# A hybrid attention and feed-forward block: another order of seven down-projection products, constant products at the start, and a later broadcast and rotary table

## The chip, the cores and the metric

The kernel runs on one core of one Trainium2 chip. The time is device microseconds (us) of one execution, from the kernel's start to its end; lower is better. The profile is that of one execution on the chip.

## The reference, cut to what matters

One layer (DEPTH is 1), 512 positions of width 2048, all float32. The products carry full float32 precision in the kernel, by way of split operands.

```python
h = rmsnorm(x, g_attn_pre)
proj = h @ w_in                       # [stick-breaking q | k | v | latents | rotary key]
o_sb  = stick_breaking_attention(q_sb, k_sb, v_sb)
o_mla = mla_attention(q_nope, apply_rope(q_rope, cos, sin), k_nope, apply_rope(k_rope, cos, sin), v)
mixed = concat(rmsnorm(o_sb), rmsnorm(o_mla))
x = x + rmsnorm(mixed @ w_o, g_attn_post)
h = rmsnorm(x, g_ffn_pre)
u = causal_depthwise_conv(h @ w_up, conv_w, conv_b)       # w_up: 2048 x 11264
gate, val = split(u)
y = (gelu(gate) * val) @ w_down                            # w_down: 5632 x 2048
x = x + rmsnorm(y, g_ffn_post)
```

## The kernel before

The engines are TensorE (PE), VectorE (DVE), ScalarE (ACT), GpSimd (POOL) and SyncE (SP, which issues loads). Every float32 operand is split into a high and a low part (`hi`, `lo`) of TensorE's rounded float32 type, and every product is three matmuls: high by high, and the two mixed ones (`three`, L119 to L122). A weight tile is loaded by an SP transfer into `wr` (raw), ScalarE casts it to `wh` (L109, L921), and VectorE subtracts to get `wl` (L111, L921). A tile framework puts each engine's instructions into a fixed order, which each engine then runs through in that order; `tc.issue_after` (wrapped as `behind`, L116) pins an instruction behind another one.

**The start.** `gen_v(0)` makes the values of the first heads: 16 k-steps of 12 matmuls, each 128x128 by 128x512, in four banks. Its weights come as two tiles of one k-step and seven of two, each k-step with a 256 KB row of the transposed x (`x_rows`), which is scaled and split into `act_hi` (ScalarE, L194) and `act_lo` (VectorE, L195). When all k-steps but the last are written, `x_squares` loads x a second time in 16 tiles `acc` (five buffers) and sums their squares on ScalarE (L201). From these come the norms: a reduction (L481), a power on GpSimd, the scales `sx` and `nsx` (L485, L486) and the diagonal tile `t` (L139). The products are made with x that isn't normed; the norm comes in when the banks are copied out (L325, L326). Then `gen_qk(0)` makes q and k of the first pair, 16 k-steps of 6 matmuls; after its first k-step, two full-float32 matmuls broadcast the norm from `t` to all partitions (`bcast`, L145, copied out by L146). `rope_tables` (L382 and on) computes cosine and sine for the rotary parts, mostly on VectorE in tiles `aT`.

**Middle.** Both attentions, `w_o`, and the up-projection. The last goes in units: a block product is made from seven block products instead of eight (`sevenfold`, L928), with sums and differences of blocks on both sides. After the last products of one unit, the left sides of the first down-projection chunk are made (`then`, in `up_steps`).

**The down-projection.** `open_down` (L1079) makes room: `act_lo` for left sides, and twenty 128x512 pages for sums: `u2`, `11`, `12`, `21` and `22`. There are five chunks (`NST`) and in each two halves `q` of the columns. In each half the seven products of `sevenfold` are made with an accumulating variant: 24 matmuls of 128x128 by 128x512 each. `quarter` loads a weight block of 1 MB on SP; `added` adds another block onto a raw tile with an accumulating transfer that GpSimd issues. `wr` has four buffers, `wh` and `wl` three. `g_side` (L1107) makes the left side of product n for a chunk out of four blocks that are loaded into `a5h` and `a5l`: a copy (ScalarE, L1123), a subtraction (VectorE, L1124), for some also a difference of blocks (VectorE, L1129). The left sides sit in `a6h` (product 1), `a6l` (2), `a3h` (5), `s6` (6; shown as `s`), `a3l` (7) and `act_lo` (3, 4). `down_steps` (L1161) names the bank pairs and what follows each product:

```python
    ORDER = (1, 2, 5, 6, 7, 3, 4)
        name = {1: "X", 2: "X", 5: "D", 3: "D", 7: "C", 4: "C", 6: "Y"}[n]
        fresh = n in (1, 5, 7, 6)
```

A fresh product overwrites its banks; products 2, 3 and 4 add onto the banks of 1, 5 and 7. After each product `add_to` (L1088) adds its banks to the pages: product 1 to `u2` (by ScalarE's copy, L1092, in the first chunk, by VectorE, L1094, later), product 2 to `11`, and so on. In half 1 of a chunk, the left side of product n of the next chunk is made right after product n.

**The end.** `open_last` (L1205) adds and subtracts `u2` to and from the pages of the other sums (twelve operations, L1219, L1223 and L1224). `last_steps` makes the last two blocks' products, in 16 groups of 12 matmuls, each taken from its bank by VectorE (L1243); then come the norm, the residual and the output.

## Time and profile before

| | |
|---|---|
| median of 3 runs | 2044.94 us (2043.98 to 2048.38) |
| profiled execution, its own time | 2040.72 us |
| span of its instructions | 2038.9 us |
| TensorE busy | 2003.2 us (98%) |
| VectorE busy | 1532.6 us (75%) |
| ScalarE busy | 924.4 us (45%) |
| mean granted TensorE clock | 0.998 of full speed |
| last matmul begins | 2027.87 us |

The span runs from the first to the last instruction. In a row of the timeline the columns are: start in us, duration in us, engine, source line, operation, output and inputs by the names in the program with their shapes, how many stand in the row, and in brackets how long the engine idled before it and what it waited for. Matmuls overlap, so their distance, not their duration, says what one costs. In the list of waits, a row gives the engine, the waiting tile and line, the releaser, and the total in us, the number of times and the longest. In a table of windows, a row gives the stretch, its length, and the busy time (with the number of instructions) of TensorE, its weight load, VectorE, ScalarE and GpSimd, then the granted clock, the share of the transfer engines and GB/s.

### The profile page before, as it was taken

What the parts mean: (1) busy time and instruction counts of PE and PEld (TensorE: products, weight loads), DVE (VectorE), ACT (ScalarE), POOL (GpSimd) and SP (SyncE); (2) the same over time, 40 slices, a digit from 0 to 9 for tenths busy, and PEclk for the clock granted to TensorE, in tenths of its full rate; (3) what the DMA queues carried; (4) which work ended last, traced back from release to release, by engine and by line L of the source; (5) the groups of instructions that cost most, each with busy time, mean ns of one, the idle gap of its engine ahead of it and who ended that gap; (6) DMA issues with size and microseconds to landing.
All of it is one profiled execution on the core that took longest, in us unless ns stands there. A gap on an engine that the chain in (4) does not pass through costs nothing.

```text
span 2038.9 us, 29849 instructions
## 1 busy us (share of the span) xinstructions
PE 2003.2 (98%) x12580; PEld 1808.4 (89%) x12580; DVE 1532.6 (75%) x1556; ACT 924.4 (45%) x1105; POOL 159.6 (8%) x192
## 2 busy tenths in 40 slices
PE   9999999999999999999999999999999999999997
PEld 7788888888888889999999999999999788878876
DVE  7454355687343888888888888888888889898886
ACT  6343244466433654454444444444444564444432
POOL 0000000123021200000000000000000000000004
PEclk9999999999999999999999999999999999999999
DMA  8422322211532524224323432343235677767772
GB/s 277 125 73 74 103 73 65 81 42 63 181 122 99 177 95 133 94 94 148 132 94 99 159 115 94 114 154 105 94 129 187 180 189 203 206 169 183 207 206 83
DMA packets 186630, 266.12 MB, mean 131 GB/s; under 512 B 8832, under 2 KB 123648, under 8 KB 185984
## 3 DMA queue, kind: packets, MB, share of 16 engines
q1 hardware_dynamic: 170704, 227.04, 34.2%
q0 software_dynamic: 15360, 36.71, 8.2%
q8 instruction: 98, 1.61, 0.3%
q10 hardware_dynamic: 432, 0.47, 0.1%
q14 instruction: 36, 0.29, 0.0%
HBM read 244.26 MB, written 19.92 MB: 130 GB/s over the span
## 4 chain that ended last, share of the span: by engine, by line
PE 82%; DVE 9%; DMA 3%; issue 3%; ACT 3%; POOL 0%; SPq 0%; DVEq 0%; ACTq 0%; POOLq 0%
PE ps L984 40%; PE ps L1156 10%; PE ps L120 9%; PE ps L121 9%; PE ps L122 9%; PE ps L270 2%; DVE wl L921 2%; ACT wh L921 1%; DMA wr<-in_w_down_dram 1%; PE ps L865 1%; DVE wr L925 1%; PE ps L246 1%; DVE act_hi L1094 1%; DVE t L452 0%; DVE wl L111 0%
## 5 line engine op out<-in xcount | busy, mean ns | idle before, releaser
L921 ACT CAST wh<-wr 128x2048 fp32r<-128x2048 f32 x220 | 419.0, 1909 | 613.5 <-DVE wr L925 274.1
L921 DVE TENSOR_TENSOR wl<-wr,wh 128x2048 fp32r<-128x2048 f32 x220 | 503.1, 2288 | 149.6 <-ACT wh L921 149.4
L984 PE MATMUL ps<-act_hi,wh 128*128 128x256 f32 x1344 | 380.4, 283 | 1.6 <-ACT wh L921 1.6
L984 PE MATMUL ps<-act_hi,wl 128*128 128x256 f32 x1344 | 380.4, 283 | 0.0
L984 PE MATMUL ps<-act_lo,wh 128*128 128x256 f32 x1344 | 380.4, 283 | 0.0
L111 DVE TENSOR_TENSOR wl<-wr,wh 128x1024 fp32r<-128x1024 f32 (+2 forms) x107 | 130.3, 1218 | 185.1 <-ACT wh L109 184.8
L984 PEld LDWEIGHTS ps<-act_hi,wh 128*128 128x128 f32 x1344 | 258.0, 192 | 1.9 <-ACT wh L921 1.8
L984 PEld LDWEIGHTS ps<-act_lo,wh 128*128 128x128 f32 x1344 | 258.0, 192 | 0.0
L984 PEld LDWEIGHTS ps<-act_hi,wl 128*128 128x128 f32 x1344 | 258.0, 192 | 0.0
L925 DVE TENSOR_TENSOR wr<-wr 128x2048 f32<-128x2048 f32 x104 | 237.7, 2286 | 1.1
L109 ACT CAST wh<-wr 128x1024 fp32r<-128x1024 f32 (+2 forms) x107 | 110.3, 1031 | 200.4 <-PE ps L121 78.3
L122 PE MATMUL ps<-wh,act_lo 128*128 128x512 f32 x400 | 156.2, 390 | 0.0
L120 PE MATMUL ps<-act_hi,wh 128*128 128x512 f32 x368 | 145.2, 395 | 0.0
L122 PE MATMUL ps<-act_hi,wl 128*128 128x512 f32 x368 | 143.4, 390 | 0.0
L121 PE MATMUL ps<-act_lo,wh 128*128 128x512 f32 x368 | 143.4, 390 | 0.0
L120 PE MATMUL ps<-wh,act_hi 128*128 128x512 f32 x352 | 138.1, 392 | 5.0 <-ACT act_hi L194 5.0
L121 PE MATMUL ps<-wl,act_hi 128*128 128x512 f32 x352 | 137.5, 391 | 0.0
L1156 PE MATMUL ps<-wh,act_lo 128*128 128x512 f32 x320 | 100.4, 389 | 0.7 <-ACT act_hi L1092 0.7
L984 PE MATMUL ps<-a5h,wl 128*128 128x256 f32 x336 | 95.2, 283 | 1.5 <-DVE wl L921 1.5
L984 PE MATMUL ps<-a6h,wl 128*128 128x256 f32 x336 | 95.1, 283 | 0.0
L984 PE MATMUL ps<-a5h,wh 128*128 128x256 f32 x336 | 95.1, 283 | 0.0
L984 PE MATMUL ps<-a3h,wh 128*128 128x256 f32 x336 | 95.1, 283 | 0.0
(392 smaller groups left out, 4351.9 us busy)
## 6 DMA issues: line engine op xcount, KB each, us to landing
wr<-in_w_up_dram SPq DMA_DIRECT2D x84, 1024.0 KB, 6.5
wr<-in_w_down_dram SPq DMA_DIRECT2D x44, 1024.0 KB, 6.9
wr<-in_w_in_dram SPq DMA_DIRECT2D x59, 512.0 KB, 3.7
wr<-in_w_down_dram POOLq DMA_DIRECT2D x20, 1024.0 KB, 9.7
wr<-in_w_o_dram SPq DMA_DIRECT2D x32, 512.0 KB, 3.6
g_dram<-v POOLq DMA_DIRECT2D x42, 256.0 KB, 6.0
a5l<-g_dram SPq DMA_DIRECT2D x5, 1024.0 KB, 11.0
a5h<-g_dram SPq DMA_DIRECT2D x5, 1024.0 KB, 8.3
```

Source lines behind the costliest of these rows:

```text
L109: sc.copy(hi, raw)
L111: ve.tensor_tensor(lo, raw, f(hi), ALU.subtract)
L120: te.matmul(ps, lh, rh, start=start, stop=False)
L121: te.matmul(ps, lh, rl, start=False, stop=False)
L122: seen["mm"] = te.matmul(ps, ll, rh, start=False, stop=stop)
L246: te.transpose(dst, a(b, j), ident)
L270: te.matmul(dst, q[:, b * P:(b + 1) * P], k[:, k0:S], start=i == 0, stop=False)
L865: mark["part"] = te.matmul(dst, l[:, kk, ms], r, start=first and kg == 0 and kk == 0 and i == 0, stop=kg == 3 and kk == 3 and i == 2, skip ...
L921: made.append((sc.copy(hi, w), ve.tensor_tensor(lo, w, f(hi), ALU.subtract)))
L925: ve.tensor_tensor(w, w, v, ALU.add)
L984: te.matmul(dst, l[:, k, ms], r[:, k, :], start=fresh and k == 0 and m == 0 and i == 0, stop=k == 7 and i == 2, skip_group_check=True)
L1156: te.matmul(bs[t], l[:, k, ts_], r[:, k, :], start=fresh and k == 0 and i == 0, stop=k == FU - 1 and i == 2, skip_group_check=True)
```

## The change

Seven edits. (1) `ones` is filled first on GpSimd, and nine products of it with itself go into a bank that nothing reads. (2) The first weights of `gen_v(0)` come as four tiles of one k-step and six of two; the raw tiles of the four lie in pages of other tags. (3) The rotary table's first operation stands behind the last `lo` of the first values, not behind `act_lo` of k-step 4. (4) Six k-steps of `gen_qk(0)` instead of one stand before the broadcast. (5) The down-projection's products come in the order 1, 5, 2, 6, 7, 3, 4. (6) The left sides of the first chunk: 1, 5 and 2 are made after products 6, 7 and 3 of the last up unit, 6 after product 1 of the first half (`open_sixth`), 7 after 5, 3 after 2, 4 after 6; before, 6, 7, 3 and 4 all came after the last product of the up unit. (7) The twelve `u2` operations of `open_last` stand behind the last `wl`.

```diff
--- before.py
+++ after.py
@@ -71,12 +71,15 @@
     def f(t):
         return t.bitcast(F32)
 
+    ones = const.tile([P, P], F32, name="ones")
+    po.memset(ones, 1.0)
+    idle = bank()
+    for _ in range(9):
+        te.matmul(idle[:, 0:P], ones, ones, start=True, stop=True)
     ident = const.tile([P, P], F32, name="ident")
     make_identity(nc, ident)
     identb = const.tile([P, P], BF16, name="identb")
     po.tensor_copy(identb, ident)
-    ones = const.tile([P, P], F32, name="ones")
-    po.memset(ones, 1.0)
     sbmask = const.tile([P, P], BF16, name="sbmask")
     po.memset(sbmask, 0.0)
     po.affine_select(out=sbmask, in_=sbmask, pattern=[[1, P]], compare_op=ALU.is_gt, fill=NEG,
@@ -102,8 +105,8 @@
     def new_raw(shape):
         return wp.tile(shape, F32, tag="wr", name="wr", bufs=2)
 
-    def load_w(src, r0, kn, c0, cols):
-        raw = new_raw([P, kn, cols])
+    def load_w(src, r0, kn, c0, cols, raw=None):
+        raw = new_raw([P, kn, cols]) if raw is None else raw
         sy.dma_start(raw, src[r0:r0 + kn * P, c0:c0 + cols].rearrange("(k p) c -> p k c", p=P))
         hi = wp.tile([P, kn, cols], R32, tag="wh", name="wh")
         sc.copy(hi, raw)
@@ -304,10 +307,11 @@
 
     def gen_v(vb, first=False):
         banks = [bank() for _ in range(NT)]
-        steps = [1, 1] + [2] * 7 if first else [2] * 8
+        steps = [1] * 4 + [2] * 6 if first else [2] * 8
         for kg, kn in enumerate(steps):
             k0 = sum(steps[:kg])
-            wh, wl = load_w(w_in, k0 * P, kn, 2 * SBW + vb * 512, 512)
+            raw = page("s" if kg < 2 else "om", 3).rearrange("p (k c) -> p k c", k=1) if kn == 1 else None
+            wh, wl = load_w(w_in, k0 * P, kn, 2 * SBW + vb * 512, 512, raw)
             if first:
                 for kk in range(kn):
                     x_rows(k0 + kk)
@@ -323,7 +327,7 @@
         for t in range(NT):
             hi, lo = pg_v(R32), pg_v(R32)
             sc.activation(hi, banks[t], AF.Copy, scale=rx[:, t:t + 1])
-            ve.scalar_tensor_tensor(lo, banks[t], rx[:, t:t + 1], f(hi), ALU.mult, ALU.subtract)
+            seen["v"] = ve.scalar_tensor_tensor(lo, banks[t], rx[:, t:t + 1], f(hi), ALU.mult, ALU.subtract)
             v_sb[vb].append((hi, lo))
 
     qk_sb = {}
@@ -386,7 +390,7 @@
         def tmp():
             return pg_at()
         ang, a1, a2 = tmp(), tmp(), tmp()
-        with behind(("lo", 4)):
+        with behind("v"):
             ve.tensor_copy(ang, posi)
         ve.tensor_scalar_mul(ang, ang, gcol(C_INVF, 0))
         m12, m22 = MAGIC * 2.0 ** 12, MAGIC * 2.0 ** 22
@@ -487,7 +491,7 @@
     run(vgen)
     rx_d = diagonals(rx)
     qk0 = gen_qk(0)
-    run(qk0, 1.0)
+    run(qk0, 7.7)
     with behind("mm"):
         rx_bc = bcast(rx_d, page("rx", 1))
     cos, ssin = rope_tables()
@@ -964,7 +968,7 @@
             return w_parts(w[11] if added else plus(w[11], w[21]))
 
         if added:
-            return p1, p2, p5, p6, p7, p3, p4
+            return p1, p5, p2, p6, p7, p3, p4
         return p1, p5, p6, p7, p2, p3, p4
 
     later = []
@@ -1052,7 +1056,7 @@
         def then(use, *ns):
             def both(w):
                 use(w)
-                if ns[0] == 6:
+                if not ns:
                     open_down()
                 for n in ns:
                     g_side(0, n)
@@ -1060,8 +1064,8 @@
             return both
 
         if unit == NFF // 2 - 1:
-            return zip(sevenfold(quarter, (8, 256)), (m1, m5, then(m6, 1), then(m7, 2), m2, then(m3, 5),
-                                            then(m4, 6, 7, 3, 4)))
+            return zip(sevenfold(quarter, (8, 256)), (m1, m5, then(m6, 1), then(m7, 5), m2, then(m3, 2),
+                                            then(m4)))
         return zip(sevenfold(quarter, (8, 256)), (m1, m5, m6, m7, m2, m3, m4))
 
 
@@ -1076,10 +1080,13 @@
     def kept(name, shape, dt=F32):
         return hp.tile([P, *shape], dt, tag=name, name=name)
 
-    def open_down():
+    def open_sixth():
         some(len(later))
         tp_stack.close()
         d["gp"], d["gpool"] = stacked("gp", side="right")
+        g_side(0, 6)
+
+    def open_down():
         d["rest"] = kept("act_lo", (16, S), R32)
         ps = pages(kept("act_hi", (16, S))) + [pg_v() for _ in range(4)]
         d["acc"] = {n: {(t, q): ps.pop(0) for q in range(2) for t in range(2)}
@@ -1156,7 +1163,7 @@
                     te.matmul(bs[t], l[:, k, ts_], r[:, k, :], start=fresh and k == 0 and i == 0,
                               stop=k == FU - 1 and i == 2, skip_group_check=True)
 
-    ORDER = (1, 2, 5, 6, 7, 3, 4)
+    ORDER = (1, 5, 2, 6, 7, 3, 4)
 
     def down_steps(ch, q):
         def rows(kh, nh):
@@ -1183,6 +1190,9 @@
             down_product(z[name], w, d["g"][n], fresh)
             if q == 1 and ch + 1 < NST:
                 g_side(ch + 1, n)
+            if first and q == 0:
+                {1: open_sixth, 5: lambda: g_side(0, 7), 2: lambda: g_side(0, 3),
+                 6: lambda: g_side(0, 4)}.get(n, lambda: None)()
             if n == 1:
                 add_to("u2", q, z["X"], first)
             elif n == 2:
@@ -1212,16 +1222,17 @@
                 ve.tensor_tensor(lo, g_, f(hi), ALU.subtract)
                 d["gh"].append((hi, lo))
         acc = d["acc"]
-        for t in range(2):
-            for q in range(2):
-                y[t, q], u2 = acc["11"][t, q], acc["u2"][t, q]
-                y[2 + t, q], y[t, 2 + q], y[2 + t, 2 + q] = acc["21"][t, q], acc["12"][t, q], acc["22"][t, q]
-                ve.tensor_tensor(y[t, 2 + q], y[t, 2 + q], u2, ALU.subtract)
-        for t in range(2):
-            for q in range(2):
-                u2 = acc["u2"][t, q]
-                ve.tensor_tensor(y[2 + t, 2 + q], y[2 + t, 2 + q], u2, ALU.subtract)
-                ve.tensor_tensor(y[2 + t, q], y[2 + t, q], u2, ALU.add)
+        with tc.issue_after(made[-1][1].ins):
+            for t in range(2):
+                for q in range(2):
+                    y[t, q], u2 = acc["11"][t, q], acc["u2"][t, q]
+                    y[2 + t, q], y[t, 2 + q], y[2 + t, 2 + q] = acc["21"][t, q], acc["12"][t, q], acc["22"][t, q]
+                    ve.tensor_tensor(y[t, 2 + q], y[t, 2 + q], u2, ALU.subtract)
+            for t in range(2):
+                for q in range(2):
+                    u2 = acc["u2"][t, q]
+                    ve.tensor_tensor(y[2 + t, 2 + q], y[2 + t, 2 + q], u2, ALU.subtract)
+                    ve.tensor_tensor(y[2 + t, q], y[2 + t, q], u2, ALU.add)
         d["ssy"] = sm.tile([P, NT, 8], F32, tag="ssy", name="ssy", bufs=2)
         ve.memset(d["ssy"], 0.0)
         d["gb"] = pages(cpage("a3h", (4, S), F32))
```

TensorE, first half of the third chunk, the border of two products. `a6h` is the left side of product 1, `a6l` of product 2, `a3h` of product 5. Before:

```order
L1156 MATMUL ps<-wl,a6h 128x512
L1156 MATMUL ps<-wh,a6h 128x512 x2
L1156 MATMUL ps<-wl,a6h 128x512
L1156 MATMUL ps<-wh,a6h 128x512
L1156 MATMUL ps<-wh,a6l 128x512
L1156 MATMUL ps<-wl,a6l 128x512
L1156 MATMUL ps<-wh,a6l 128x512 x2
```

Now:

```order
L1163 MATMUL ps<-wl,a6h 128x512
L1163 MATMUL ps<-wh,a6h 128x512 x2
L1163 MATMUL ps<-wl,a6h 128x512
L1163 MATMUL ps<-wh,a6h 128x512
L1163 MATMUL ps<-wh,a3h 128x512
L1163 MATMUL ps<-wl,a3h 128x512
L1163 MATMUL ps<-wh,a3h 128x512 x2
```

Product 5 stands between product 1 and product 2, which writes the same banks as product 1. In every half of every chunk the 24 matmuls of product 5 are now in one piece; before, in most halves they stood in part before and in part behind those of product 2.

ScalarE, from the last rows of x (`act_hi<-o,gv`) on to the first copies of the values (`v<-ps,rs`); L201 and, now, L204 are the squares, L109 and L112 the weight casts. Before:

```order
L109 CAST wh<-wr 128x1024 x2
L194 ACTIVATE act_hi<-o,gv 128x512 x3
L201 ACTIVATE acc,ssx<-acc 128x512 x2
L109 CAST wh<-wr 128x1024
L201 ACTIVATE acc,ssx<-acc 128x512 x5
L109 CAST wh<-wr 128x1024
L201 ACTIVATE acc,ssx<-acc 128x512 x9
L692 DMA gvc<-in_taps_dram 128x352
L109 CAST wh<-wr 128x1024 x2
L325 ACTIVATE v<-ps,rs 128x512
```

Now:

```order
L197 ACTIVATE act_hi<-o,gv 128x512 x3
L112 CAST wh<-wr 128x1024
L197 ACTIVATE act_hi<-o,gv 128x512
L204 ACTIVATE acc,ssx<-acc 128x512 x16
L696 DMA gvc<-in_taps_dram 128x352
L112 CAST wh<-wr 128x1024 x2
L329 ACTIVATE v<-ps,rs 128x512
```

All 16 squares stand in a row before the first weight of pair 0. VectorE has, in the same manner, the reduction, the scales and `t` before its first two subtractions for pair 0, and SP the 16 loads of `acc` before the weight loads of pair 0.

VectorE at the end, from the last accumulating products to the first takes (L1243, now L1254). Before:

```order
L921 TENSOR_TENSOR wl<-wr,wh 128x2048
L1219 TENSOR_TENSOR act_hi<-act_hi 128x512
L1094 TENSOR_TENSOR v<-v,ps 128x512 x2
L1219 TENSOR_TENSOR act_hi<-act_hi 128x512
L1224 TENSOR_TENSOR v<-v,act_hi 128x512
L921 TENSOR_TENSOR wl<-wr,wh 128x2048
L1224 TENSOR_TENSOR v<-v,act_hi 128x512
L1243 TENSOR_TENSOR act_hi<-ps,act_hi 128x512 x4
```

Now:

```order
L925 TENSOR_TENSOR wl<-wr,wh 128x2048
L1101 TENSOR_TENSOR v<-v,ps 128x512 x2
L925 TENSOR_TENSOR wl<-wr,wh 128x2048
L1230 TENSOR_TENSOR act_hi<-act_hi 128x512 x4
L1234 TENSOR_TENSOR act_hi<-act_hi 128x512
L1235 TENSOR_TENSOR v<-v,act_hi 128x512
L1234 TENSOR_TENSOR act_hi<-act_hi 128x512
...
L1234 TENSOR_TENSOR act_hi<-act_hi 128x512
L1235 TENSOR_TENSOR v<-v,act_hi 128x512
L1254 TENSOR_TENSOR act_hi<-ps,act_hi 128x512 x5
```

The subtractions and additions of the `u2` pages are now all behind the last `wl`.

## Rows read from the trace of the kernel before

**Rows 1.** The page's first lines: the span, and each engine's busy time.

```profile
span 2038.9 us, 29849 instructions
PE 2003.2 (98%) x12580; PEld 1808.4 (89%) x12580; DVE 1532.6 (75%) x1556; ACT 924.4 (45%) x1105; POOL 159.6 (8%) x192
```

**Rows 2.** The waits of TensorE, grouped by waiting line and releaser.

```profile
PE ps L1156 <- DVE act_hi L1094: 5.0, 6, 1.1
...
PE ps L1156 <- DVE wl L921: 5.0, 2, 2.9
...
PE ps L145 <- DVE t L139: 3.2, 2, 1.7
...
PE ps L1156 <- ACT act_hi L1092: 1.7, 2, 1.0
...
PE ps L1156 <- ACT wh L921: 0.3, 1, 0.3
```

**Rows 3.** Timeline of TensorE, down-projection, lines L1156.

```profile
1603.62 0.50 PE L1156 MATMUL ps<-wl,a3h 128*128 128x512 f32 x1 [2.87 <-DVE wl L921]
...
1753.63 0.47 PE L1156 MATMUL ps<-wh,a6l 128*128 128x512 f32 x1 [1.11 <-DVE act_hi L1094]
...
1764.61 0.39 PE L1156 MATMUL ps<-wh,s 128*128 128x512 f32 x1
...
1951.06 0.49 PE L1156 MATMUL ps<-wl,a3h 128*128 128x512 f32 x1 [2.16 <-DVE wl L921]
```

**Rows 4.** Timeline of TensorE, the first 54 us.

```profile
5.03 0.79 PE L120 MATMUL ps<-wh,act_hi 128*128 128x512 f32 x1 [5.03 <-ACT act_hi L194]
...
8.14 0.39 PE L121 MATMUL ps<-wl,act_hi 128*128 128x512 f32 x1
...
50.24 0.39 PE L120 MATMUL ps<-act_hi,wh 128*128 128x512 f32 x1
...
53.30 1.10 PE L145 MATMUL ps<-t,ones 128*128 128x512 f32 x2 [1.54 <-DVE t L139]
```

**Rows 5.** Timeline of GpSimd, the start.

```profile
0.86 0.20 POOL L79 MEMSET ones<- 128x128 f32 x1
```

**Rows 6.** Matmul groups by shape: count, then busy us and mean ns.

```profile
L246 PE MATMUL ps<-ident,s 128*128 128x128 f32 x120 | 15.1, 273 | 0.0
```

**Rows 7.** Timeline of ScalarE, first, eighth, thirteenth and last square of x.

```profile
32.64 0.62 ACT L201 ACTIVATE acc<-acc 128x512 f32<-128x512 f32 x1
...
42.70 0.62 ACT L201 ACTIVATE acc<-acc 128x512 f32<-128x512 f32 x1
...
46.36 0.63 ACT L201 ACTIVATE acc<-acc 128x512 f32<-128x512 f32 x1
...
49.66 0.64 ACT L201 ACTIVATE acc<-acc 128x512 f32<-128x512 f32 x1 [0.30 <-DMA acc<-in_x_dram]
```

**Rows 8.** Timeline of VectorE, the norms after the squares.

```profile
50.41 0.18 DVE L481 TENSOR_REDUCE ssr<-ssx 128x4 f32<-128x16 f32 x1
...
52.47 0.69 DVE L139 TENSOR_TENSOR t<-ident,rs 128x512 f32<-128x512 f32 x1
...
53.07 0.69 DVE L408 SCALAR_TENSOR_TENSOR aT<-aT 128x512 f32<-128x512 f32 x1
...
53.67 1.22 DVE L111 TENSOR_TENSOR wl<-wr,wh 128x1024 fp32r<-128x1024 f32 x1
```

**Rows 9.** Windows: one chunk of the down-projection, both halves.

```profile
1753.00:1832.00 79.00, 76.75 (x336) 62.92 (x336) 71.02 (x70) 34.43 (x29) 5.14 (x4) 1.00 0.70 188
```

**Rows 10.** Timeline of VectorE, down-projection, a weight and the end.

```profile
1762.16 2.29 DVE L921 TENSOR_TENSOR wl<-wr,wh 128x2048 fp32r<-128x2048 f32 x1 [0.26 <-ACT wh L921]
...
1936.59 1.29 DVE L1223 TENSOR_TENSOR act_hi<-act_hi 128x512 f32<-128x512 f32 x2
...
1988.79 2.28 DVE L921 TENSOR_TENSOR wl<-wr,wh 128x2048 fp32r<-128x2048 f32 x1
```

**Rows 11.** The page's transfers: issuer, count, KB each, median us to landing.

```profile
a5l<-g_dram SPq DMA_DIRECT2D x5, 1024.0 KB, 11.0
```

## Prediction

> **What bounds the kernel now.** The page's first lines [rows 1] say it: TensorE is busy for 2003.2 of 2038.9 us, so every gain has to come out of the 35.7 us in which it isn't, or out of matmuls that run slower than they need. Next I read TensorE's waits [rows 2]. The down-projection, line 1156, lost 5.0 us in six waits for an addition to the `u2` pages (L1094), 5.0 us in two waits for a `wl`, and 1.7 and 0.3 us in three waits on ScalarE: 12.0 us in all. The broadcast matmuls, line 145, lost 3.2 us in two waits. Then the places [rows 3]: in a steady half of a chunk the matmul that waits is the first of product 2 (left side `a6l`), 1.11 us at 1753.63; the two long waits are for `wl` of product 5 (`a3h`), 2.87 us in the first chunk and 2.16 us in the last. Last the start [rows 4]: the first matmul begins at 5.03, the eighth at 8.14, the 193rd (the first of q/k pair 0) at 50.24. So the later 185 intervals took 0.2276 us each and the first seven 0.444 us each, about twice that. This is how the lower of TensorE's two levels, 1.2 GHz, looks beside 2.4 GHz, after an engine that had done nothing. At 53.30 the broadcast waited 1.54 us.
>
> **Part 1, nine constant products.** Seven intervals at 0.444 instead of 0.2276 us lost 3.11 - 1.59 = 1.5 us. If the nine products are what raises the clock, those 1.5 us come back. `ones` is ready early: its memset takes 0.20 us and began at 0.86 [rows 5]; now it is the first on that queue. Nine products of the same size took 0.273 us each elsewhere [rows 6]; a product of constants in full float32 is two instructions on this engine, as the broadcast's is [rows 4]. So nine take between 2.5 us and, at the lower level with two instructions each, some 9 x 2 x 0.273 = 4.9 us. From about 1.0 us they end between 3.5 and 5.9, against 5.03 when the first true product may start. The bounds are -0.9 us (they end late and the clock isn't up) and +1.5 us. Before, the clock rose 3.1 us after the first matmul; 1.0 + 3.1 = 4.1 lies before 5.03, so I take the gain: **1.5 us**.
> The Trainium skill, "TensorE: Matmul & The Clock Gate", Part 1, says that the throttled state is the default and that its release is not timed from a kernel's first matmul, so that the number of slow matmuls differs from run to run (6, 11 or 14 in its example). By that the term is anything between 0 and 1.5 us and the sum below between 11.5 and 13.0; the trace has a single start, and cannot tell.
>
> **Part 2, the first 75 us.** Two things change order. The broadcast moves from behind one k-step of q/k pair 0 to behind six, five k-steps of 6 x 0.2276 us or 6.8 us later. Its input `t` must only come within these, so its **1.54 us** go [rows 4]. But the squares of x now stand in a row before the first weight of pair 0 on ScalarE, their 16 loads in a row before that weight on SyncE, and on VectorE the statistics and `t` before its `wl`. Before, TensorE began pair 0 at 50.24 while the chain of the statistics was still running: last square at 49.66 [rows 7], sum at 50.41, `t` at 52.47 [rows 8]. Now pair 0 waits for that chain. After the last square's start the chain took 53.67 + 1.22 - 49.66 = 5.2 us to the end of the next `wl`, of which 0.6 us was a rotary operation that now comes later: 4.6 us. When does the last square start? The first began at 32.64. `acc` has five pages, so each load waits for the square five before it: 42.70 to 46.36 is one such round of five, 3.66 us; before, with other loads between, the 15 steps took 17.0 us or 5.7 a round [rows 7]. Three rounds of 3.66 end at 43.6, three of 5.7 at 49.7. `wl` is then ready between 48.2 and 54.3. TensorE, 1.5 us early, wants it at its second matmul, 48.97. So the new wait is between 0 and 5.3 us. No weight load lies between these loads any more, so I take a value near the quick end: **-0.7 us**.
> The four extra raw pages of `gen_v` let the first loads go out sooner; TensorE waited nowhere in this product, so 0. The rotary table's operations (one is the 0.69 us at 53.07 [rows 8]) now all run from about 55 us on; the table is used first by the latent stage after all of the first attention, and the `wl` between them are needed every 5.5 us only: 0.
>
> **Part 3, order 1, 5, 2.** Products 1 and 2 share one bank pair. Product 2 can't overwrite it before VectorE has added product 1 to `u2`. With product 5 between, TensorE has 24 x 0.2276 = 5.5 us of other work, against two additions of 0.6 us and whatever stands before them on VectorE; the six waits of at most 1.1 us [rows 2] fit in. **5.0 us**. What is late next? Product 5 now comes first, so its weight sum (`plus`, L925) and its `wl` (2.3 us [rows 10]) are needed 5.5 us sooner. Both SyncE loads come in the changed order too, and the two accumulating loads that GpSimd issues get one more product's time in the case of `w12`. So they should be on time; but VectorE works 71.02 of 79.0 us there [rows 9]. A chunk without waits is 2 x 7 x 24 x 0.2276 = 76.5 us, which leaves it 5.5 us. And some `wl` are just in time already: the one that ends at 1764.45 [rows 10] is used from 1764.61 [rows 3].
>
> **Part 4, left sides of the first chunk spread.** The 2.87 us at 1603.62, the 1.7 us on ScalarE's copies of `act_hi` and 0.3 us on a cast come from a heap of splits before the first weights. Spread over the last up unit's products and the first down products they stand behind work of 5.5 us each: **4.9 us**.
>
> **Part 5, the twelve `u2` operations behind the last `wl`.** Before, six of them ran in the last chunk's first half, from 1936.59 on [rows 10], 0.6 us each and 3.6 us together, ahead of the late `wl` for 1951.06: **2.2 us**. All twelve now stand behind the `wl` that began at 1988.79, 7.2 us in which the final takes wait, some 5 us more than before. TensorE fills a bank with 12 products there, 2.73 us, and has eight banks, so it wants the first one back only after 21.8 us; VectorE has little but the takes to do in these 43.7 us and has caught up before the last: 0.
>
> **The sum.** 1.5 + 1.54 - 0.7 + 5.0 + 4.9 + 2.2 = 14.4 us (the last three are the 12.0 of [rows 2], rounded up by 0.1). For new waits at `wl` that are just in time I set 0.14 us in each of the ten halves, the slack of 0.16 us seen above, 1.4 us. It leaves 13.0 us. The profiled execution took 2040.72, so its like would take 2027.7; the median of the runs before is 4.2 us above it, 2044.94, and I carry the difference over: **2032.0**. Bounds: 15.1 us if no new wait comes (2029.8), 8.5 us if the square chain costs its upper bound and the rest holds (2036.4).
>
> **Rivals.** (a) **The squares arrive as late as before.** Pair 0 waits 5.3 us instead of 0.7: 2032.0 + 4.6 = 2036.6. For it: five pages, 5.7 us a round before. Against: those rounds held weight loads.
> (b) **The clock isn't raised** by nine small products of constants: without 1.5 us, 2033.5. This is also the case that a part of the change doesn't do what it says.
> (c) **VectorE becomes the bound.** If its own idle time per chunk, 79.0 - 71.0 = 8 us [rows 9], can't shrink because it is waiting at the head of its queue for loads and casts, the steady halves gain nothing, and the six waits (5.0 us) come back elsewhere: 2037.0. With 2.2 us of the last chunk too it is 2039.2.
> (d) **Slower: the left sides of the next chunk block VectorE.** `a5l` lands 11.0 us after its issue [rows 11]. A subtraction that needs it stands in VectorE's queue; if the new order brings VectorE there earlier, each `wl` behind it is late. To end slower by over 0.2% this has to cost 13.0 + 4.1 = 17 us, some 3.4 us in each of five chunks; if all must fit into two products' 10.9 us, of which a `wl` of 2.3 and two additions of 0.6 leave 7.4, it lacks 3.6 us each time, 18 us, and the time is 2032.0 + 18 = 2050. Against: before, such a load cost TensorE nothing in steady chunks.
> The Trainium skill, same page, Part 1, "Architectural detail", calls ScalarE's and VectorE's queues strictly first in, first out, which is the rule by which (d) would work; the waits of [rows 2] on `wl` agree with it.
>
> **How the numbers follow.** The forecast holds 0.58, (a) 0.14, (b) 0.10, (c) 0.13, (d) 0.05. A measurement of this kernel tells 0.2%, 4.1 us, from no change. The forecast, (a) and (b) are faster by more; of (c) about half. Of (c) the other half, 0.07, is the same. So faster 0.88, same 0.07, slower 0.05. The forecast's own range is 2029.5 to 2034.5. The range takes in (a), (b) and the first form of (c): 2028.5 to 2038.5; (d), the rest of (c) and a few cases of runs that scatter lie outside.
>
> **What would show it.** Right: matmuls 0.23 us apart from the first true product on; no wait at the broadcast; a wait under 2 us at the first `wl` of pair 0; line 1156's successor with under 3 us of waits, none of them for the additions; the stretch behind TensorE's last matmul as long as before. Wrong: a wait of 4 us or more near 49 us (a), 0.44 us spacing from 5 us on (b), VectorE's waits for `wh` unchanged and TensorE's waits for `wl` in each half (c), or a `wl` behind a subtraction on `a5l` in each chunk (d).

## The result and the profile after

The changed kernel takes 2031.16 us (median of 4 runs, 2030.33 to 2031.95); the kernel before 2044.46 us (4 runs beside it). The ratio over all runs, which is not that of the two medians, is 0.9931, with an interval of 0.9914 to 0.9949. By the medians it is faster by 13.3 us; 2032.0 had been forecast, with a range of 2028.5 to 2038.5.

The two profiled executions differ by less: spans of 2029.7 and 2038.9 us, 9.2 us. This gap of 4 us between medians and profiles is half of the story below.

The page of the kernel after, its opening lines:

```profile
span 2029.7 us, 29907 instructions
...
PE 2003.5 (99%) x12598; PEld 1811.7 (89%) x12598; DVE 1533.1 (76%) x1557; ACT 925.2 (46%) x1106; POOL 159.8 (8%) x192
```

TensorE's busy time is nearly the same, 0.3 us more: it runs the same matmuls and the nine new products, 18 instructions. (One product in full float32 counts as two; the broadcast too is one product in two instructions.) Its waits in groups, which answer to [rows 2]; L1163 was L1156, L988 the up-projection's L984, L148 the broadcast's L145:

```profile
PE ps L1163 <- DVE wl L925: 3.4, 4, 1.6
PE ps L988 <- DVE wl L925: 3.3, 2, 2.2
PE ps L148 <- DVE t L142: 1.7, 1, 1.7
...
PE ps L125 <- DVE wl L114: 0.5, 1, 0.5
```

The 12.0 us in eleven waits of the down-projection have become 3.4 us in four. None is for an addition. One broadcast wait of 1.7 us is left, that of the second attention, which the change didn't touch; the first is gone. The second row is a loss: before, this line waited 1.5 us in one place.

```profile
PE ps L984 <- DVE wl L921: 1.5, 1, 1.5
```

TensorE's timeline after, at the start and at the places of the losses:

```profile
0.98 3.65 PE L78 MATMUL ps<-ones 128*128 128x128 f32 x18 [0.98 <-POOL ones L75]
5.30 0.50 PE L123 MATMUL ps<-wh,act_hi 128*128 128x512 f32 x1 [0.67 <-ACT act_hi L197]
5.63 0.39 PE L124 MATMUL ps<-wl,act_hi 128*128 128x512 f32 x1
5.86 0.40 PE L123 MATMUL ps<-wh,act_hi 128*128 128x512 f32 x1
...
50.45 0.50 PE L125 MATMUL ps<-act_hi,wl 128*128 128x512 f32 x1 [0.52 <-DVE wl L114]
...
58.30 1.02 PE L148 MATMUL ps<-t,ones 128*128 128x512 f32 x2
...
738.64 0.39 PE L988 MATMUL ps<-act_hi,wl 128*128 128x256 f32 x1 [2.21 <-DVE wl L925]
...
1835.28 0.39 PE L1163 MATMUL ps<-wh,s 128*128 128x512 f32 x1
1837.22 0.50 PE L1163 MATMUL ps<-wl,s 128*128 128x512 f32 x1 [1.56 <-DVE wl L925]
1837.56 0.63 PE L1163 MATMUL ps<-wh,s 128*128 128x512 f32 x2
```

From the first true product on, matmuls are 0.23 us apart: no slow ones. Pair 0 waits 0.52 us for its `wl`, and the broadcast at 58.30 not at all. The longest new wait of the down-projection is 1.56 us, at product 6 (`s`). Around it one sees what a wait costs: 1835.28 to 1837.56 is 2.28 us for two matmuls that else take 0.46, so 1.82 us are lost where the row says 1.56. I call the 0.26 us more the restart; around the other waits of the down-projection that stand alone it is 0.24 to 0.34 us.

Where the 9.2 us of the profiles lie, from the beginnings of the first and last matmul of each stage:

| stage | before, us | after, us | difference |
|---|---|---|---|
| start to the first matmul of the up-projection | 737.64 | 736.04 | -1.60 |
| up-projection, to the first down product | 850.32 | 852.43 | +2.11 |
| down-projection, to the first product of the last units | 396.62 | 385.53 | -11.09 |
| last units, to the last matmul's beginning | 43.29 | 43.29 | 0 |
| behind that | 11.03 | 12.41 | +1.38 |

The matmuls that begin these stages, before and then after (the last row is the last matmul; before, it began at 2027.87):

```profile
737.64 0.28 PE L984 MATMUL ps<-act_hi,wh 128*128 128x256 f32 x1
...
1587.96 0.40 PE L1156 MATMUL ps<-wh,a6h 128*128 128x512 f32 x1
...
1984.58 0.39 PE L120 MATMUL ps<-wh,act_lo 128*128 128x512 f32 x1
```

```profile
736.04 0.28 PE L988 MATMUL ps<-act_hi,wh 128*128 128x256 f32 x1
...
1588.47 0.40 PE L1163 MATMUL ps<-wh,a6h 128*128 128x512 f32 x1
...
1974.00 0.39 PE L123 MATMUL ps<-wh,act_lo 128*128 128x512 f32 x1
...
2017.29 0.39 PE L125 MATMUL ps<-wh,act_lo 128*128 128x512 f32 x1
```

In the down-projection 8.6 us of waits and seven restarts of 0.26 us (1.8 us) went, 10.4 of the 11.1 us. In the up-projection 1.8 us of waits and one restart came, 2.1 us.

### The profile page after: what moved, and what is told of

Read it like the earlier page. It is cut to its first block, busy times and chain, and to the rows that moved or that the text cites. A ratio compares the mean times of both kernels' runs of the same rounds, so it can differ in the third digit from the quotient of the medians.

```text
span 2029.7 us, 29907 instructions
## 1 busy us (share of the span) xinstructions
PE 2003.5 (99%) x12598; PEld 1811.7 (89%) x12598; DVE 1533.1 (76%) x1557; ACT 925.2 (46%) x1106; POOL 159.8 (8%) x192
## 4 chain that ended last, share of the span: by engine, by line
PE 87%; DVE 6%; DMA 3%; ACT 2%; issue 1%; POOL 0%; SPq 0%; DVEq 0%; ACTq 0%; POOLq 0%
PE ps L988 41%; PE ps L1163 15%; PE ps L123 9%; PE ps L125 9%; PE ps L124 9%; PE ps L273 2%; PE ps L869 1%; DMA a5l<-g_dram 1%; DMA wr<-in_w_in_dram 1%; DVE wl L925 1%; PE ps L249 1%; ACT wh L925 1%; DVE wr L929 1%; DMA acc<-in_x_dram 1%; DVE act_hi L1101 0%
## 5 line engine op out<-in xcount | busy, mean ns | idle before, releaser
L988 PE MATMUL ps<-act_hi,wl 128*128 128x256 f32 x1344 | 380.5, 283 | 2.2 <-DVE wl L925 2.2
L988 PE MATMUL ps<-act_hi,wh 128*128 128x256 f32 x1344 | 380.4, 283 | 1.6 <-ACT wh L925 1.6
L988 PE MATMUL ps<-act_lo,wh 128*128 128x256 f32 x1344 | 380.3, 283 | 0.0
L988 PEld LDWEIGHTS ps<-act_hi,wl 128*128 128x128 f32 x1344 | 258.0, 192 | 2.4 <-DVE wl L925 2.4
L988 PEld LDWEIGHTS ps<-act_hi,wh 128*128 128x128 f32 x1344 | 258.0, 192 | 1.9 <-ACT wh L925 1.8
L988 PEld LDWEIGHTS ps<-act_lo,wh 128*128 128x128 f32 x1344 | 258.0, 192 | 0.0
L114 DVE TENSOR_TENSOR wl<-wr,wh 128x1024 fp32r<-128x1024 f32 (+1 forms) x104 | 127.8, 1229 | 171.1 <-ACT wh L112 170.7
L112 ACT CAST wh<-wr 128x1024 fp32r<-128x1024 f32 (+1 forms) x104 | 108.1, 1039 | 194.0 <-PE ps L125 69.9
L1163 PE MATMUL ps<-wh,act_lo 128*128 128x512 f32 x320 | 100.1, 389 | 0.0
L988 PE MATMUL ps<-a5h,wl 128*128 128x256 f32 x336 | 95.2, 283 | 1.1 <-DVE wl L925 1.1
L988 PE MATMUL ps<-a5h,wh 128*128 128x256 f32 x336 | 95.1, 283 | 0.0
L988 PE MATMUL ps<-a3h,wh 128*128 128x256 f32 x336 | 95.1, 283 | 0.0
L988 PE MATMUL ps<-a3l,wh 128*128 128x256 f32 x336 | 95.1, 283 | 0.0
```

Of the source, the lines that this page charges most:

```text
L112: sc.copy(hi, raw)
L114: ve.tensor_tensor(lo, raw, f(hi), ALU.subtract)
L988: te.matmul(dst, l[:, k, ms], r[:, k, :], start=fresh and k == 0 and m == 0 and i == 0, stop=k == 7 and i == 2, skip_group_check=True)
L1163: te.matmul(bs[t], l[:, k, ts_], r[:, k, :], start=fresh and k == 0 and i == 0, stop=k == FU - 1 and i == 2, skip_group_check=True)
```

## Experiments

**The kernel before again, and the nine products on it.** The profile of before was faster (2040.72) than each of its four unprofiled runs. I wanted to know what a second one shows, and what the nine constant products do alone.

> The kernel before, unchanged, for a second profile and more single runs: its profiled execution took 2040.72 us, its other four 2043.4 to 2048.4, while the changed kernel's four lie within 2030.3 to 2032.0. Theory A (the scatter is the start: TensorE's clock rises at another moment in each run): this profile shows more than seven slow matmuls at the start or a later first matmul, and the lost time of the start explains the difference to 2040.72. Theory B (the scatter lies in the down-projection, in waits for loads that come late): the start is as before, 1.5 us, and the waits of line 1156 add up to more than 12 us. Both: same time as before, ratio 1.000 within 0.002.

Measured: median 2044.72 of 11 runs, 2040.11 to 2048.61, ratio 1.0003 (0.9994 to 1.0013). The start took eleven slow matmuls instead of seven, and pair 0 began at 51.12 instead of 50.24, as theory A has it. But of the 1.6 us between the two spans only 0.75 lie ahead of the up-projection. The down-projection took 397.4 us, 0.8 more than before, though its waits are a little shorter. The reason stands in TensorE's timeline of this run and in its window (columns: stretch, length, busy time of PE, PEld, DVE, ACT, POOL, granted clock, transfer share, GB/s):

```profile
1604.37 0.79 PE L1156 MATMUL ps<-wl,a3h 128*128 128x512 f32 x1 [2.84 <-DVE wl L921]
1604.96 0.63 PE L1156 MATMUL ps<-wh,a3h 128*128 128x512 f32 x1
1605.39 0.63 PE L1156 MATMUL ps<-wl,a3h 128*128 128x512 f32 x1
```

```profile
1600.00:1610.00 10.00, 7.16 (x25) 5.48 (x24) 8.60 (x8) 4.50 (x4) 0.00 (x0) 0.83 0.64 238
```

Behind the wait of 2.84 us the matmuls are 0.43 us apart and the granted clock of this stretch is 0.83: TensorE ran at 1.2 GHz for a part of it and lost (1 - 0.83) x 10 = 1.7 us. In the first profile of before, behind the same wait (2.87 us, [rows 3]), the clock of this stretch was 1.00. So the clock fell behind a wait of this length in one execution and not in the other. Neither theory had this.

```diff
+    ones = const.tile([P, P], F32, name="ones")
+    po.memset(ones, 1.0)
+    idle = bank()
+    for _ in range(9):
+        te.matmul(idle[:, 0:P], ones, ones, start=True, stop=True)
...
```

> Only the nine constant products in the first us. Theory A: faster by 4 us or more in the median, and the single runs lie within 2 us of each other as those of the changed kernel do. Theory B: faster by the 1.5 us of seven slow matmuls less 0.3 us by which the first true product came later, 1.2 us in the profile, and the runs scatter as before. In both the matmuls are 0.23 us apart from the first true product on, and the broadcast still waits (3 us, as TensorE reaches it earlier).

Measured: 2046.16 (11 runs, 2042.41 to 2049.40), ratio 1.0011 (1.0002 to 1.0020). No gain, slower by a tenth of a per cent; both theories fell. The first products did run at 0.23 us. But 45 us later it is all lost. TensorE's timeline and window of this run:

```profile
52.29 0.50 PE L123 MATMUL ps<-act_hi,wh 128*128 128x512 f32 x1 [2.22 <-ACT wh L112]
...
54.63 0.79 PE L125 MATMUL ps<-act_hi,wl 128*128 128x512 f32 x1 [1.41 <-DVE wl L114]
55.22 0.63 PE L123 MATMUL ps<-act_hi,wh 128*128 128x512 f32 x1
```

```profile
50.00:60.00 10.00, 6.36 (x15) 3.87 (x15) 7.66 (x15) 3.44 (x6) 1.12 (x1) 0.66 0.53 145
...
1950.00:1960.00 10.00, 7.26 (x27) 5.41 (x26) 10.00 (x11) 1.23 (x1) 0.23 (x1) 0.87 0.95 230
1960.00:1970.00 10.00, 10.00 (x37) 8.08 (x36) 5.84 (x5) 3.81 (x2) 1.29 (x1) 0.79 0.42 127
```

With another program at the start the framework also made another order there: all 16 squares and their loads stand ahead of pair 0's first weight, as in the changed kernel. But the last square begins at 49.69, not at 45.86. ScalarE in this run, then in the kernel after:

```profile
49.69 0.63 ACT L204 ACTIVATE acc<-acc 128x512 f32<-128x512 f32 x1 [0.78 <-DMA acc<-in_x_dram]
```

```profile
45.86 0.63 ACT L204 ACTIVATE acc<-acc 128x512 f32<-128x512 f32 x1 [0.78 <-DMA acc<-in_x_dram]
```

So TensorE waits 3.6 us in two steps for pair 0's `wh` and `wl`, and the clock falls (0.66 over ten us, 3.4 us lost). This is rival (a), with a price on top. It also means that this run isn't the clock edit alone. The wait of 2.05 us in the last chunk is followed by another fall (0.87 and 0.79), and one of 2.86 us in the first chunk by a third. This profiled execution is the slowest of the eleven (2049.40), so three falls in one are not the rule. The Trainium skill, "TensorE: Matmul & The Clock Gate", section "Why this matters for your kernels", warns that idle gaps make the clock fall back, and says in Part 1 that the moment isn't tied to the kernel. On the moment the traces agree: a gap of 2.84 us (the kernel before again) stands with a fall, one of 2.87 us (before) without. On the gaps they go further: the page warns of longer ones than the 2.05 and 2.84 us behind which the clock fell here, and the measurement decides.

**The middle of the change alone.** Order and left sides, with the start and the end as before.

```diff
-            return p1, p2, p5, p6, p7, p3, p4
+            return p1, p5, p2, p6, p7, p3, p4
...
+            if first and q == 0:
+                {1: open_sixth, 5: lambda: g_side(0, 7), 2: lambda: g_side(0, 3),
+                 6: lambda: g_side(0, 4)}.get(n, lambda: None)()
```

> The order 1, 5, 2, 6, 7, 3, 4 and the spread left sides of the first chunk, with the start and the end as before. My theory: the waits for additions to u2 (5.0 us), those of the first chunk (4.9 us) and nothing else go; 2.2 us before product 5 of the last chunk stay or shrink; new waits on wl of 2 to 4 us as in the changed kernel: 6 to 9 us faster in the profile, ratio 0.996. Rival (the gain of the change lies mostly at the start): 3 us or less.

Measured: 2031.14 (5 runs, 2030.88 to 2034.72), ratio 0.9945 (0.9931 to 0.9958), span 2029.1: as fast as the whole change. The rival falls, and the gain is above my 6 to 9 us: 9.8 in the profiles. The waits of the down-projection are those of the whole change, and the 2.2 us at product 5 of the last chunk are gone although the twelve `u2` operations are free:

```profile
PE ps L1159 <- DVE wl L921: 3.4, 4, 1.5
```

The down-projection took 385.7 us, the last units 43.9, 0.6 more than before, and the stretch behind the last matmul 11.1 us, as before. The start had 14 slow matmuls and pair 0 began at 51.76. The up-projection begins 2.1 us later than in the whole change. So there the start's gain is paid out again by the two losses, +2.1 and +1.4 us.

Only the order, with the left sides of the first chunk made all at once, as before:

```diff
-            return p1, p2, p5, p6, p7, p3, p4
+            return p1, p5, p2, p6, p7, p3, p4
...
-    ORDER = (1, 2, 5, 6, 7, 3, 4)
+    ORDER = (1, 5, 2, 6, 7, 3, 4)
```

> Only the order 1, 5, 2, 6, 7, 3, 4; the left sides of the first chunk stay in a heap. My theory: the six waits for additions to u2 go, the first chunk keeps waits of some 3 to 5 us, so the down-projection (first product to the first of the last units) takes 389 to 391 us, against 396.6 before and 385.7 with order and sides. The wait of over 2 us that stays lets the granted clock fall in some of the runs, so they scatter by 3 us or more, and the median is 2035 to 2038. Rival (the heap was harmful only with the old order): down-projection under 387 us, median 2031 to 2033.

Measured: 2038.27 (8 runs, 2035.79 to 2041.21), ratio 0.9971 (0.9961 to 0.9981). The down-projection took 393.0 us, 2 us above what I had expected, as the sides made at once now cause one long wait, at product 2, with a fall of the clock behind it:

```profile
1605.13 0.50 PE L1156 MATMUL ps<-wl,a6l 128*128 128x512 f32 x1 [4.10 <-DVE wl L921]
```

```profile
1600.00:1610.00 10.00, 5.90 (x19) 4.44 (x18) 8.64 (x9) 4.29 (x5) 0.00 (x0) 0.83 0.80 288
```

By the ratios, the order is worth 0.29% or 6 us and the spread sides, added to it, another 0.26%, 5 us; no run has the sides alone.

**The wait at 738.64.** The first `wl` of the up-projection takes the place of `wh` and `wl` buffers of the stages before; ten first weight tiles instead of nine move the round of these buffers. In the kernel after, VectorE waits there for the last matmul of the stage before:

```profile
736.30 2.29 DVE L925 TENSOR_TENSOR wl<-wr,wh 128x2048 fp32r<-128x2048 f32 x1 [5.34 <-PE ps L869]
```

```diff
-        steps = [1] * 4 + [2] * 6 if first else [2] * 8
+        steps = [1] * 6 + [2] * 5 if first else [2] * 8
...
-            raw = page("s" if kg < 2 else "om", 3).rearrange("p (k c) -> p k c", k=1) if kn == 1 else None
+            raw = page("s" if kg < 3 else "om", 3).rearrange("p (k c) -> p k c", k=1) if kn == 1 else None
```

> The changed kernel with the first weights in eleven tiles (six of one k-step, five of two) instead of ten, which moves the round of wh and wl buffers by one. The changed kernel lost 2.2 us at 738.64, where the first wl of the up-projection waits for a matmul that still reads the buffer whose place it takes. My theory (the tenth tile of edit 2 moved that round): the 2.2 us at the first wl of the up-projection go, and the profiled span is 1.5 to 2.2 us under the changed kernel's 2029.7, ratio to the kernel before about 0.992. Rival (the wait has to do with the earlier arrival of TensorE there, 1.6 us): it stays at 1.6 us or more, span 2029 to 2030.

Measured: 2033.7 (5 runs, 2033.06 to 2034.25), ratio 0.9951 (0.9939 to 0.9964), span 2031.0: slower than the kernel after, all five runs above the nine of that kernel, though the intervals of the ratios overlap. VectorE's `wl` no longer waits for that matmul, but now ScalarE's `wh` does:

```profile
735.43 1.90 ACT L925 CAST wh<-wr 128x2048 fp32r<-128x2048 f32 x1 [5.84 <-PE ps L869]
```

And TensorE waits for both:

```profile
737.38 0.39 PE L988 MATMUL ps<-act_hi,wh 128*128 128x256 f32 x1 [1.81 <-ACT wh L925]
739.71 0.58 PE L988 MATMUL ps<-act_hi,wl 128*128 128x256 f32 x1 [1.82 <-DVE wl L925]
```

The expected gain didn't come; that the buffers' round decides who waits there agrees with it. So I took edit 2 back:

```diff
-        steps = [1] * 4 + [2] * 6 if first else [2] * 8
+        steps = [1, 1] + [2] * 7 if first else [2] * 8
...
-            raw = page("s" if kg < 2 else "om", 3).rearrange("p (k c) -> p k c", k=1) if kn == 1 else None
+            raw = None
```

> The changed kernel without its second edit: the first weights again in nine tiles (1, 1, 2, ...) through wr alone. The first wl of the up-projection then takes the place of a buffer that TensorE reads last 24 matmuls earlier. My theory: the wait of 2.2 us there shrinks under 0.4 us, the next one stays at 1.1 to 1.5 us; at the start the wait before pair 0 grows by 0 to 3 us, since the loads of the first product are held up as before. Span 2027.5 to 2030. Rival (the second edit pays at the start by more than it costs): span over 2030.5.

Measured: 2030.82 (5 runs, 2028.55 to 2032.13), ratio 0.9932 (0.9919 to 0.9944), span 2026.8. The wait is gone; `wl` begins as soon as its cast is done, and the next wait is the old one:

```profile
732.60 2.29 DVE L925 TENSOR_TENSOR wl<-wr,wh 128x2048 fp32r<-128x2048 f32 x1 [1.11 <-ACT wh L925]
```

The price at the start is small: pair 0 waits 0.82 us, where the kernel after waits 0.52. In the single runs it can't be told from the kernel after.

**The pin of the twelve operations.** Edit 7 taken back.

> The changed kernel without its last edit: the twelve operations on the u2 pages may stand where the framework puts them. My theory: the stretch behind TensorE's last matmul is 11.0 to 11.1 us as before, against 12.4 in the changed kernel; the last chunk waits at most 0.6 us more; span 0.8 to 1.4 us shorter, 2028.3 to 2028.9, median 2030.0. Rival (the last chunk needs the pin): the 2.2 us wait at product 5 of the last chunk comes back, span 2030.5 or more.

Measured: 2031.07 (5 runs, 2030.52 to 2031.61), ratio 0.9934 (0.9921 to 0.9948), span 2029.8. Both expectations fell: the stretch behind the last matmul took 11.8 us, between the two; the last units wait 0.64 us once for a `wl` and take 44.2 us instead of 43.3; the 2.2 us did not come back. The edit neither pays nor costs in the time.

The stretch behind the last matmul, in all twelve profiles, goes by two edits, the pin and the number of first weight tiles:

| | `u2` operations free | pinned |
|---|---|---|
| nine first tiles | 11.0 to 11.1 us (six profiles) | 11.8 us (old tiles) |
| ten or eleven | 11.8 us (this run) | 12.4 to 12.6 us (four profiles) |

Each of the two edits costs 0.7 us there, and the costs add up. The part of the pin can be seen in the profile after, on VectorE and GpSimd:

```profile
2019.26 1.35 DVE L1287 TENSOR_TENSOR act_hi<-act_hi,a3h 128x512 f32<-128x512 f32 x1 [0.85 <-ACT v L1255]
```

```profile
2018.79 1.28 POOL L1287 TENSOR_TENSOR v<-v,a3h 128x512 f32<-128x512 f32 x1
```

Two multiplications with two operands from SBUF each run at the same time, and VectorE's takes 1.35 us instead of 0.69. Before, and in the last run below, GpSimd's was done before VectorE's began. In all five pinned profiles VectorE's four multiplications of this line took 0.88 to 1.63 us, in the seven others 0.69 to 0.71. Why the tiles cost 0.7 us so late stays open.

**The change without the nine products.**

> The changed kernel without the nine constant products. My theory: seven to thirteen slow matmuls at the start (1.5 to 2.8 us), of which 0.5 us is hidden, as pair 0 waits that long for its wl in the changed kernel: median 2032 to 2033.5 and a scatter of 1 to 2 us. Rival (the start is bound by the chain of the squares in any case): within 0.5 us of 2031.2.

Measured: 2033.84 (5 runs, 2031.92 to 2034.68), ratio 0.9946 (0.9933 to 0.9958). Thirteen matmuls are slow at the start, pair 0 begins at 51.60 and no longer waits. The up-projection begins at 737.64, 1.6 us later than in the kernel after. The nine products are worth 2.7 us here by the medians, 1 to 3 us by the ratios of the two runs of the kernel after; the intervals overlap. They can be worth this if the squares come early: the last one starts at 45.86 in the kernel after and at 48.03 here, instead of 49.66 [rows 7]. Which edit brings them forward isn't shown: no run takes back the later rotary table or the later broadcast alone.

**The kernel after again, and the two edits taken back together.**

> The changed kernel, unchanged, on the same chip as the next run and with more single runs. Theory (its one wait of over 2 us, 2.21 at the first wl of the up-projection, lets the clock fall in some runs): the runs lie between 2028.5 and 2034, those at a granted clock of 0.998 lower than those at 0.997 or less by 1 to 2 us. Rival (no falls in this kernel): all within 1 us.

Measured: 2031.14 (5 runs, 2030.84 to 2032.13), ratio 0.9940 (0.9928 to 0.9952). The clock did fall in the profiled run (0.97 and 0.86 in the two stretches from 730 to 750):

```profile
730.00:740.00 10.00, 7.79 (x38) 6.50 (x38) 4.66 (x5) 6.05 (x7) 0.00 (x0) 0.97 0.66 210
740.00:750.00 10.00, 10.00 (x75) 10.00 (x75) 9.95 (x9) 3.77 (x3) 0.99 (x2) 0.86 0.07 27
```

Yet the down-projection began only 0.12 us later than in the profile without a fall: the next wait there, 1.13 us, had gone in return, as VectorE sets the pace at that place, busy for 9.95 of the ten us. The profiles without the pin and without the nine products show a fall there too, and in all four the up-projection took 852.4 us. So this fall costs nothing in the time. My 1 to 2 us were too much; the runs lie within 1.3 us.

```diff
-        steps = [1] * 4 + [2] * 6 if first else [2] * 8
+        steps = [1, 1] + [2] * 7 if first else [2] * 8
...
-        with tc.issue_after(made[-1][1].ins):
...
```

> The changed kernel without its second and its seventh edit (first weights in nine tiles through wr; the u2 operations unpinned), the best guess from the runs so far. Theory: no wait of over 2 us is left, so the clock stays up after the start; up-projection as in the run with the old tiles; the stretch behind the last matmul 11.0 to 11.8 us and up to 1 us of waits in the last chunk: 2028 to 2031, 0.5 to 2 us faster than the changed kernel. Rival (the two edits only trade places): within 0.5 us of it.

Measured: 2029.97 (5 runs, 2028.95 to 2034.13), ratio 0.9939 (0.9923 to 0.9955), span 2027.2. The wait in the up-projection is away, the end takes 11.1 us, and VectorE's multiplication there its old time:

```profile
2018.06 0.69 DVE L1286 TENSOR_TENSOR act_hi<-act_hi,a3h 128x512 f32<-128x512 f32 x1 [0.85 <-ACT v L1254]
```

Its span is 2.5 us under that of the kernel after; in the medians the gain is 1.2 us, and the intervals overlap. It may be the best version; that isn't shown. One execution took 2034.13, so scatter is left. That no wait of over 2 us remains isn't enough to keep the clock up: with eleven tiles it fell to 0.87 over ten us behind the two waits of 1.81 and 1.82 us. At the start of this profile, as in that with the old tiles, the first three intervals are slow in spite of the nine products:

```profile
5.21 0.80 PE L123 MATMUL ps<-wh,act_hi 128*128 128x512 f32 x1
5.80 0.63 PE L124 MATMUL ps<-wl,act_hi 128*128 128x512 f32 x1
6.22 0.48 PE L123 MATMUL ps<-wh,act_hi 128*128 128x512 f32 x1
6.54 0.40 PE L124 MATMUL ps<-wl,act_hi 128*128 128x512 f32 x1
```

## Why the prediction was right, and where it wasn't

The time was right, 2031.16 for 2032.0, but its sum was not: of the 13.0 us that it forecast for the profile, 9.2 came. The rest of the 13.3 us lies outside what the one profile of before shows. Of the prediction's own signs of being right, three came (the spacing from the first true product on, no wait at the broadcast, under 2 us at pair 0's `wl`) and two did not: the down-projection waited 3.4 us instead of under 3, though not for the additions, and the stretch behind the last matmul is longer. Point by point:

- **The clock, 1.5 us.** Right in kind, no slow matmul is left in this profile; in two of the seven with these products three are, so the full gain isn't certain. Pair 0 begins 1.05 us earlier. In the other profiles without the products the start took eight to fourteen slow matmuls, so more can be gained there. The run with the nine products on the start of before gained nothing, but the squares stand ahead of pair 0 there too, and late. That the term counts only as far as the squares are early enough fits both runs; no run shows it by itself.
- **The broadcast, 1.54 us, and the squares, -0.7 us.** Right: no wait, and 0.52 us and a restart in place of 0.7. The last square began at 45.86, between the bounds of 43.6 and 49.7. As the step has it, no weight load lies between the squares' loads any more. In the run with the nine products alone one still does, behind the first: the second of the squares' loads is issued at 29.36, and at 25.61 in the kernel after. But the run with the old tiles has one at the same place, and its last square begins at 46.72, so this isn't all. (Pair 0 takes `wl` at its third matmul, not at its second, as the step says; that is 0.23 us.) Rival (a) did not come; it did in the run with the nine products alone, with 3.6 us.
- **Order, 5.0 us, and sides, 4.9 us.** Right: no wait for an addition, none in the first chunk. What was left out is the restart of 0.26 us per wait.
- **The `u2` operations, 2.2 us.** The wait went, but for another reason than the step gave: it goes without this edit, and already with the order alone. The edit itself was priced at 0 at the end and costs 0.7 us there, where VectorE's last multiplications meet GpSimd's.
- **New waits, -1.4 us.** Too small: 3.4 us and restarts, in four places, where ten had been assumed. They are at `wl` of products 5 and 6, as rival (c) would have it, but too few to make VectorE the bound. The 0.14 us per half were no more than a guess, and the slack of 0.16 us behind them was misread: the matmul at 1764.61 takes `wh`, and the first with that `wl` begins at 1764.84. With the restarts left out of the savings too, the down-projection came out 0.4 us better than forecast.
- **Nothing in between.** The step that set the new tiles of the first weights at 0 failed: the up-projection, 690 us later, waits 2.2 us because a buffer's place is read later, and the end takes another 0.7 us.
- **"I carry the difference over"**, 4.2 us between the profiled execution of before and the median. This failed too: the profiled execution after lies 0.4 us above its median. The profile of before was one with few slow matmuls and no fall of the clock. In 53 executions of before beside these runs, 2039.8 to 2048.6 us, the time goes with the granted clock: 2040.0 us in the mean of 2 at 0.999, 2042.3 of 15 at 0.998, 2044.3 of 21 at 0.997, 2045.7 of 15 at 0.996 or less. Their mean is 2043.9, at 0.997, where the profile has 0.998. An estimate from this is that falls make 0.001 of 2044 or 2 us of the 3.2 between them. The slow matmuls of the start don't show in this clock: it is 1.00 over the first ten us of before. They are a second part; the rest is open, as executions at the same 0.998 differ by up to 5 us. The long waits that the change takes away (2.87 and 2.16 us) are places of falls in the profiles of the kernel before again and of the nine products alone. In the changed kernel the one fall seen costs nothing, and its nine executions lie within 1.8 us. So the change gained some 4 us on top of its profile, which my sum didn't hold; that falls are the larger part is argued, not shown. How many each unprofiled execution had stays open; only the profiles show places.

On one side stand errors of 2.1, 1.4 and some 0.7 us (the start) too much, less 0.4 in the down-projection; on the other some 4 us that no term of the sum has. That they cancelled to within 1 us is luck.

## What to carry to other kernels

A wait of two or three microseconds on TensorE costs its row, a restart, and at times 1.7 to 3.4 us at the lower clock, where TensorE sets the pace; taking such waits away can gain more in the median than in a profile that happened to show no fall. Compare the granted clocks of several executions before carrying one profile's sum over to a median. Another number of tiles in an early stage can move the buffers of a late one, so look at the first wait of each later stage, and at the end, before calling the rest unchanged.

## What the runs showed of the hardware that I hadn't expected

- Single waits of TensorE of 2.05 to 4.10 us were followed by a fall to 1.2 GHz in some executions and not in others. The 2.21 us at the first `wl` of the up-projection had none in the kernel after (granted clock 1.00 from 740 to 750) and one in after again (0.86), without the pin (0.88) and without the nine products (0.83).
- Without the nine products of constants in the first us, 7 to 14 matmuls at the start were slow. With them it was at most the first interval in five profiles, and three in the other two (old tiles, and the last run).
- A wait on TensorE costs 0.26 us more than its idle time (0.24 to 0.34 around single waits of the down-projection).
- VectorE's multiplication of two SBUF operands took up to 1.63 us instead of 0.69 while GpSimd ran the same kind.
